# A decoder block on one core: the next group's front traced ahead of the recurrence's loop, adaLN's rows tied to chain operations with a third buffer, and loads respread

## The chip, the cores and the metric

The kernel runs on one core of a Trainium2 chip. The core's engines run side by side and meet only through semaphores: TensorE (PE in the profile, with its weight loads as PEld) multiplies matrices from SBUF into PSUM, VectorE (DVE) and ScalarE (ACT) do elementwise work, GpSimd (POOL) does some elementwise work off to the side, and SyncE (SP) issues every DMA of this kernel from one queue. The metric is the device time of one execution in microseconds. Before the change it is 2329.66 us, the median of three runs from 2323.95 to 2334.65.

## What is computed

One decoder block on x of 512 tokens by 2048 channels, all in float32. A normalised input, scaled and shifted by adaLN rows of a condition vector c, goes through one input projection into two mixers: an RWKV-7 recurrence over 16 heads of 64, and causal pooling with windows 2, 4, 8 and 16. Both outputs meet in one output projection. A gated MLP with a short convolution follows, and a last norm.

```python
mod = c_act @ w_ada[l] + b_ada[l]
sh1, sc1, gt1, sh2, sc2, gt2 = jnp.split(mod[:, None, :], N_MOD, axis=-1)
h = _rmsnorm(x, norm1_g[l]) * (1.0 + sc1) + sh1
p = h @ w_in[l]
y_rwkv = _rwkv7_mixer(p[..., :N_RWKV_COLS], ...)
y_pool = _pool_mixer(p[..., N_RWKV_COLS:], pool_w[l], pool_b[l], pool_scale[l])
mix = jnp.concatenate([y_rwkv, y_pool], axis=-1) @ w_out[l]
x = x + gt1 * mix
h = _rmsnorm(x, norm2_g[l]) * (1.0 + sc2) + sh2
x = x + gt2 * _conv_ffn(h, w_up[l], conv_w[l], conv_b[l], w_down[l])
```

## The kernel before

Activations lie transposed, 128 channels by 512 tokens to a tile. Weights and activations are split into a high part (`whi`, cast by ACT, line 122) and a remainder (`wlo`, subtracted by DVE, line 124), and a product is three matmuls (lines 128 to 130). Weights pass through four shared buffers `wraw`.

**The opening.** Sixteen steps over the channels project the pool inputs, sixteen more (`feed`, line 260) project eight tiles into the eight PSUM banks `pf`: one for the decay and rate inputs (`xwa`), two for the gate (`xg`), and five of the first r, k and v tiles. Lines 280 to 301 apply the token shift to each (`shift`: an ACT copy with a scale, then a DVE multiply and add) and take tanh and sigmoid of the first three. When the `pf` banks are free, their space becomes the banks of the recurrence: two single ones (`mm`), two double ones (`bt`) and a double one (`ch`).

**The recurrence.** The 16 heads go in four groups g of four heads. For each group:

- `front` (406): decay and rate from `xwa` (lines 420, 421), sigmoids, a scan, exponentials, and the norm of the keys.
- `rest` (462), a generator that stops at each `yield`. Its first part makes the operands `ar`, `bt`, the masked scores `sb` and `sk` (lines 485, 544), the token-major copies, and a small triangular solve on DVE (lines 556 to 566) whose result comes back through DRAM into `X`. The second part has two level steps (584 to 605: product, mask `pm`, add into `X`, add into `Y`), then the chain of eight dependent steps (620 to 649), then `y`. The third part, the tail, normalises `y`, applies the gate (lora weights `lg` and `gw`, 681 to 693) and stores two mix tiles.

While a group runs, PE fills its time with the input projection of the next group's six tiles (`win_some`, 703): r, k and v for two column tiles each. Each is shifted into a buffer `spill`, stored to DRAM, and reloaded by `load_cells` (716) when its place is free. Also in between are the pool groups (`pool`, 312), with weights `pw`, and 24 adaLN rows per group (`ada_rest`, 372): each is a 512 KB load into a tile `war` and one DVE product with a sum (line 381). Each of 48 rows is taken in two halves, which makes 96 products in all.

**Order.** Every instruction has a priority by its place in the source; `tc.high_priority` raises that of a block (the recurrence by 100000, pools and fronts by 50000). A scheduler lays out each engine's order before the kernel runs, taking at each time the ready instruction of highest priority. `in_step` (113) ties an adaLN row to an earlier instruction: it may not be placed ahead of it. Before, that is the last matmul of a projection block (`beats`), spread evenly over the group's blocks.

**After the recurrence.** The fourteen mix tiles that are ready are loaded and split (`load_mix`, 765) into the places of the normalised input H, the first ten output tiles are projected from them (772 to 782), and when the last group has its two mix tiles the rest follows with the residual (`x2` loads in 867 to 870, `residual` in 821).

## Time and profile before

| | |
|---|---|
| runs (three) | 2323.95, 2329.66, 2334.65 us |
| profiled execution | 2332.65 us, its span 2330.9 us |
| PE busy | 2202.7 us (95%) |
| PE weight loads | 1878.0 us (81%) |
| DVE busy | 1512.6 us (65%) |
| ACT busy | 925.9 us (40%) |
| POOL busy | 403.3 us (17%) |
| HBM read, written | 364.56 MB, 34.09 MB |

The span is the time from the first to the last instruction that the profile shows; the execution's own time is 1.75 us more. Opening, recurrence with output projection, and MLP follow one another: the four recurrence groups lie between about 215 and 730 us, the output projection's first stage goes to 795. A matmul's end is modelled, so busy shares of PE are an upper view, and its idle time is the surer reading.

### The profile page before, as it was taken

The numbers are of one execution on the slowest core, as the hardware profiler recorded it, in microseconds if no ns is written. First come the engines' busy times: TensorE is split into PE (matmuls) and PEld (weight loads), VectorE is DVE, ScalarE is ACT, GpSimd is POOL, SyncE is SP. The second block draws the span as 40 slices with busy tenths as digits, with TensorE's granted clock in tenths as the row PEclk, the third lists the DMA queues.
The fourth block names the chain that finished last, engine by engine and source line by source line (L and its number), as shares of the span: only waits on it lengthen the run. The fifth ranks groups of instructions, "written<-read, shape, count | busy, mean of one in ns | idle before, by whom it ended". The sixth has DMA issues, their size and how long they took to land.

```text
span 2330.9 us, 41813 instructions
## 1 busy us (share of the span) xinstructions
PE 2202.7 (95%) x16306; PEld 1878.0 (81%) x16306; DVE 1512.6 (65%) x2536; ACT 925.9 (40%) x1551; POOL 403.3 (17%) x390
## 2 busy tenths in 40 slices
PE   7999898888879898999999999999999999999997
PEld 5776666565657798899999999999999788888887
DVE  7896767685865669776656666656666444464457
ACT  4435242332523255544344434443444333343333
POOL 0000000000000005634434333344343000000000
PEclk9999999999989999999999999999999999999999
DMA  9884556566655775433333333333333766666555
GB/s 348 301 307 132 164 181 184 166 202 197 209 177 171 266 224 166 149 108 119 123 109 123 109 115 112 110 117 122 109 122 105 232 202 200 198 199 205 163 165 177
DMA packets 197465, 401.41 MB, mean 172 GB/s; under 512 B 37521, under 2 KB 49553, under 8 KB 193041
## 3 DMA queue, kind: packets, MB, share of 16 engines
q1 hardware_dynamic: 197266, 398.73, 54.0%
q8 instruction: 128, 2.10, 0.4%
q14 instruction: 71, 0.58, 0.1%
HBM read 364.56 MB, written 34.09 MB: 171 GB/s over the span
## 4 chain that ended last, share of the span: by engine, by line
PE 60%; DVE 2%; DMA 2%; ACT 0%; issue 0%; SPq 0%; DVEq 0%; ACTq 0%
PE b L130 20%; PE b L128 20%; PE b L129 20%; DVE wlo L124 1%; DMA wraw<-wdn 1%; DMA wraw<-wout 1%; DVE hl L159 0%; DVE x L1089 0%; ACT whi L122 0%; DVE acc L819 0%; DMA ald<-actd 0%; DVE h L157 0%; DMA x<-part 0%; DMA x<-x2d 0%; DVE x L823 0%
## 5 line engine op out<-in xcount | busy, mean ns | idle before, releaser
L122 ACT CAST whi<-wraw 128x512 fp32r<-128x512 f32 (+1 forms) x594 | 360.4, 609 | 820.8 <-DMA wraw<-wup 254.8
L124 DVE TENSOR_TENSOR wlo<-wraw,whi 128x512 fp32r<-128x512 f32 (+1 forms) x578 | 406.5, 705 | 270.9 <-ACT whi L122 263.1
L128 PE MATMUL b<-ah,whi 128*128 128x512 f32 (+1 forms) x980 | 350.0, 357 | 8.2 <-ACT whi L122 7.3
L130 PE MATMUL b<-ah,wlo 128*128 128x512 f32 (+1 forms) x980 | 349.5, 357 | 6.0 <-DVE wlo L124 5.8
L129 PE MATMUL b<-al,whi 128*128 128x512 f32 (+1 forms) x980 | 348.7, 356 | 0.0
L130 PE MATMUL b<-hh,wlo 128*128 128x512 f32 (+1 forms) x640 | 237.8, 372 | 6.0 <-DVE wlo L124 5.8
L128 PE MATMUL b<-hh,whi 128*128 128x512 f32 (+1 forms) x640 | 238.2, 372 | 0.0
L129 PE MATMUL b<-hl,whi 128*128 128x512 f32 (+1 forms) x640 | 237.8, 372 | 0.0
L128 PEld LDWEIGHTS b<-ah,whi 128*128 128x128 f32 x980 | 186.0, 190 | 36.6 <-ACT whi L122 10.8
L130 PEld LDWEIGHTS b<-ah,wlo 128*128 128x128 f32 x980 | 186.0, 190 | 34.4 <-DVE wlo L124 7.7
L129 PEld LDWEIGHTS b<-al,whi 128*128 128x128 f32 x980 | 186.1, 190 | 26.0
L984 DVE TENSOR_TENSOR pl<-raw,ph 128x768 fp32r<-128x768 f32 x104 | 105.4, 1014 | 153.0 <-ACT ph L983 153.0
L128 PE MATMUL mm<-ah,whi 128*128 128x512 f32 x444 | 183.3, 413 | 10.1 <-ACT whi L122 10.1
L130 PE MATMUL mm<-ah,wlo 128*128 128x512 f32 x444 | 183.8, 415 | 3.2 <-DVE wlo L124 3.2
L129 PE MATMUL mm<-al,whi 128*128 128x512 f32 x444 | 182.4, 411 | 0.0
L972 POOL TENSOR_TENSOR sums<-sums,raw 128x256 f32<-128x256 f32 x104 | 107.5, 1033 | 417.0 <-DVE sl L984 411.1
L130 PE MATMUL b<-tk,sl 128*128 128x256 f32 x624 | 176.7, 283 | 0.0
L129 PE MATMUL b<-tk,sh 128*128 128x256 f32 x624 | 176.5, 283 | 0.0
L128 PE MATMUL b<-tk,sh 128*128 128x256 f32 x624 | 176.0, 282 | 0.0
L983 ACT CAST ph<-raw 128x768 fp32r<-128x768 f32 x104 | 86.3, 830 | 165.9 <-PE b L129 159.5
L381 DVE SCALAR_TENSOR_TENSOR war<-war,cq 128x1024 f32<-128x1024 f32 x96 | 116.9, 1220 | 47.3 <-DMA war<-ada 47.2
L971 POOL TENSOR_TENSOR sums<-raw 128x512 f32<-128x512 f32 x104 | 135.8, 1305 | 66.9 <-DMA raw<-wups 33.1
(277 smaller groups left out, 4699.8 us busy)
## 6 DMA issues: line engine op xcount, KB each, us to landing
raw<-wups SPq DMA_DIRECT2D x104, 512.0 KB, 3.5
war<-ada SPq DMA_DIRECT2D x96, 512.0 KB, 4.4
wraw<-wdn SPq DMA_DIRECT2D x192, 256.0 KB, 3.2
wraw<-wup SPq DMA_DIRECT2D x160, 256.0 KB, 3.6
wa<-ada SPq DMA_DIRECT2D x32, 1024.0 KB, 7.5
wraw<-win SPq DMA_DIRECT2D x108, 256.0 KB, 4.1
ald<-actd SPq DMA_DIRECT2D x88, 256.0 KB, 2.7
wraw<-wout SPq DMA_DIRECT2D x78, 256.0 KB, 4.2
```

The lines of the kernel that those rows point to most:

```text
L122: mark[0] = S.copy(hi[:, 0:w], raw[:, 0:w]).ins
L124: mark[1] = eng.tensor_tensor(lo[:, 0:w], raw[:, 0:w], hi[:, 0:w].bitcast(F32), op=ALU.subtract).ins
L128: PE.matmul(ps, wh, xh, start=start, stop=False)
L129: PE.matmul(ps, wh, xl, start=False, stop=False)
L130: return PE.matmul(ps, wl, xh, start=False, stop=stop)
L381: op = V.scalar_tensor_tensor(wa, wa, 1.0, cq[0], op0=ALU.mult, op1=ALU.mult, accum_out=modq[:, kq, j : j + 1])
L971: G.tensor_tensor(sa, raw[:, 1:3, :], raw[:, 0:1, :].to_broadcast([P, 2, W2]), op=ALU.add)
L972: G.tensor_tensor(sb2[:, 0, :], sa[:, 0, :], raw[:, 2, :], op=ALU.add)
L983: act = S.copy(hi[:, sl, :], t)
L984: dve = V.tensor_tensor(lo[:, sl, :], t, hi[:, sl, :].bitcast(F32), op=ALU.subtract)
```

## The change

1. All eight shifts come first, tanh after the fourth; sigmoids and casts of the gate inputs follow when the banks are released.
2. `front` is cut in two, `front` and `key_norm`. A new `yield` in `rest` stands ahead of the chain's eight steps, and the next group's front is traced there. Of the next group's projections k comes first, then r, then the loads of both, and v is traced behind the chain.
3. In the last group that projects (g = 2), `win_two` projects both v tiles together, four channel tiles of the one and then of the other, and shifts them from PSUM straight into V. Twelve mix loads are traced right behind `win_two`, the last two behind the tail.
4. An adaLN row is tied to a DVE operation of its own group's recurrence instead of to a projection block: `spots` collects one to four places at each of the front's subtraction, the key norm, the masks, the triangular solve, the level masks, seven chain steps, and the tail. The `war` tiles have three buffers.
5. `spill`, `lg` and `rc` have one buffer where they had two; the pool weights lie in the places of `lg` and `gw` instead of in a `war` buffer.
6. Each residual tile `x2` is loaded behind the projection that needs it, instead of sixteen in a row ahead of the first.

```diff
+            for i in range(2):
+                shift(pf[1 + i], 25 + i, xg[:, i, :])
+            for i, (t, x, m) in enumerate(((0, 0, 0), (1, 0, 8), (2, 0, 16), (0, 1, 1), (1, 1, 9))):
+                shift(pf[3 + i], m, two(rkv0[t])[:, x, :])
+                if i == 0:
+                    S.activation(xwa[0:64, :], xwa[0:64, :], AF.Tanh)
+            ps0ctx.close()
...
+            def sigmoids():
+                for i in range(2):
+                    S.activation(xg[:, i, :], xg[:, i, :], AF.Sigmoid)
+                    S.copy(xgh[i], xg[:, i, :])
...
-        t = ra.tile([P, 2 * T], F32, tag="war", name="pw", bufs=2)
...
+        pw = [ra.tile([P, 2, P], F32, tag="lg", name="pw"), ra.tile([P, 3, P], F32, tag="gw", name="pw")[:, 0:2, :]]
+        for i in range(2):
+            nc.sync.dma_start(pw[i], a["poolw"][gi, :, i, :].rearrange("p (d w) -> p d w", d=2))
...
+    spots = [[] for _ in range(NQ)]
...
+        for n, spot in zip(range(n0, n1), spots[n0 // 24]):
...
-            wa = ra.tile([P, 2 * T], F32, tag="war", name="war", bufs=2)
+            wa = ra.tile([P, 2 * T], F32, tag="war", name="war", bufs=3)
...
-            i = at + (n - n0) * b // (n1 - n0)
-            if i < len(beats):
-                in_step(op, beats[i])
-        first_beat[0] = len(beats)
+            in_step(op, spot)
...
+        sb, dve = scores("b", bt)
+        spots[g] += [dve.ins] * 2
...
+        spots[g] += [dve.ins] * 2
         psb = batch()
...
+        dve = V.tensor_copy(xyl[:, 0, :, :], xyl[:, 1, :, :].rearrange("p i j -> p j i"))
+        spots[g] += [dve.ins] * 4
...
+            dve = V.tensor_tensor(rows(pm), wide(ps).rearrange("p (s t) -> p s t", t=C),
                             mlev[:, lev : lev + 1, :].to_broadcast([P, 2 * NK, C]), op=ALU.mult)
+            spots[g].append(dve.ins)
...
         S.copy(flat(xv), wide(ps))
+        yield
...
+                R = ra.tile([P, 2, C], F32, tag="rc", name="rc")
+                dve = V.tensor_add(R, pc[:, :, 0:C], xv[:, :, c, :])
+                spots[g].append(dve.ins)
...
+            lw = ra.tile([P, 2, P], F32, tag="lg", name="lg")
...
+    def win_two(pairs, i):
+        pss = [mmtile() for _ in pairs]
+        for k0 in range(0, KT, WC // P):
+            k1 = k0 + WC // P
+            for p, ps in zip(pairs, pss):
+                project(ps, a["win1"][3 + 3 * p + i - 8, :, k0 * P : k1 * P], H[k0:k1], start=k0 == 0, stop=k1 == KT)
+        return pss
...
+        if more:
+            win_some(pairs, (0,))
+            with lower():
                 r, k = load_cells(g + 1, (0, 1))
         with hp():
             next(quad)
+        if more:
+            with lower():
+                fr = key_norm(g + 1, k, front(g + 1))
+        with hp():
+            next(quad)
+        if g < NQ - 2:
+            win_some(pairs, (2,))
+        elif more:
+            pss = win_two(pairs, 2)
+            with lower():
+                for i in range(NM - 2):
+                    load_mix(i)
         with hp():
             next(quad, None)
+            if more:
+                if g < NQ - 2:
+                    rkv = [r, k] + load_cells(g + 1, (2,))
+                else:
+                    v = cell("V", "v")
+                    for x in range(2):
+                        shift(pss[x], 16 + pairs[x], two(v)[:, x, :])
+                    rkv = [r, k, v]
+        if g == NQ - 2:
+            with lower():
+                for i in range(NM - 2, NM):
+                    load_mix(i)
...
-    for i in range(NM):
-        load_mix(i)
...
+    def load_x2(f):
         t = rx.tile([P, T], F32, tag=f"x2_{f}", name=f"x2_{f}")
         nc.sync.dma_start(t, part[f] if f < NW else a["xT"][:, f, :])
         x2.append(t)
+
     for f in range(NW):
         ps = bank()
         project(ps, a["wout"][f, :, NM * P :], M[NM:])
+        load_x2(f)
         residual(f, ps, mod[:, 32 + f : 33 + f], acc, 0, T, f == 0)
```

## The prediction

> **What bounds the kernel now.** I began with the page (PE busy for 95% of the span), then cut the span into stages with the view of windows, to see where TensorE (PE) is not busy. The columns are the stretch, its length, then busy time and instructions of PE, its weight loads, DVE, ACT and POOL, the granted clock, the DMA share and GB/s.

> ```profile
> 205.00:215.00 10.00, 5.38 (x20) 1.45 (x19) 5.95 (x9) 8.67 (x15) 0.95 (x1) 0.83 0.06 16
> 215.00:730.00 515.00, 447.39 (x5974) 322.04 (x5974) 354.52 (x649) 184.13 (x310) 2.86 (x3) 0.95 0.59 179
> 730.00:795.00 65.00, 65.00 (x286) 53.23 (x284) 43.33 (x73) 18.82 (x34) 0.00 (x0) 1.00 0.73 235
> 795.00:820.00 25.00, 17.64 (x71) 13.69 (x71) 17.20 (x31) 10.46 (x21) 0.00 (x0) 0.86 0.80 274
> ```

> The change touches only what lies between 205 and 820. There PE idles 4.62 us at the switch from the input projections to the recurrence, 515.00 - 447.39 = 67.61 us in the four recurrence groups, nothing from 730 to 795, and 7.36 us where the residual tiles are loaded: 79.6 us. Outside those holes PE works, so the change can only gain what it takes out of these 79.6 us. The view of waits for PE between 205 and 820 says who ended the holes (total, times, longest):

> ```profile
> PE mm L128 <- ACT whi L122: 10.1, 2, 9.8
> PE bt L588 <- DVE X L599: 8.7, 3, 3.7
> PE bt L656 <- DVE Y L605: 7.1, 4, 2.7
> PE bt L483 <- DVE ar L475: 6.2, 3, 3.4
> PE b L130 <- DVE wlo L124: 4.5, 1, 4.5
> PE bt L420 <- DVE r L269: 4.5, 1, 4.5
> PE bt L495 <- DVE sb L485: 4.5, 3, 1.5
> PE bt L531 <- DVE sb L485: 4.0, 4, 1.1
> PE bt L495 <- DMA v<-sp: 2.8, 2, 2.0
> ```

> Most of it is DVE: a matrix product stands at the head of PE's queue, its operand comes late from DVE, and the projection work behind it can't pass. Each term below is one of these rows.

> **Part 1, adaLN's rows (three buffers, tied to chain operations).** This row of the page is the load of a row's product on DVE:

> ```profile
> L381 DVE SCALAR_TENSOR_TENSOR war<-war,cq 128x1024 f32<-128x1024 f32 x96 | 116.9, 1220 | 47.3 <-DMA war<-ada 47.2
> ```

> 96 rows of 1.22 us, and 47.2 us in which DVE stands still at a row whose 512 KB have not landed. What that does is seen in the level step of the first group (timeline: start, length, instruction, and in brackets the idle time before it and what ended it):

> ```profile
> 283.38 0.28 PE L597 MATMUL bt<-pm,Y 64*64 64x64 f32 x2
> 283.45 2.08 PE L603 MATMUL bt<-Y,pm 64*64 64x64 f32 x63
> 284.21 1.23 DVE L381 SCALAR_TENSOR_TENSOR war<-war,cq 128x1024 f32<-128x1024 f32 x1 [4.99 <-DMA war<-ada]
> 285.53 1.23 DVE L381 SCALAR_TENSOR_TENSOR war<-war,cq 128x1024 f32<-128x1024 f32 x1
> 286.68 1.22 DVE L599 TENSOR_TENSOR X<-X,bt 128x1024 f32<-128x1024 f32 x1
> 287.95 0.29 PE L588 MATMUL bt<-X,sb 64*64 64x64 f32 x4 [2.43 <-DVE X L599]
> ```

> The add into X needs only the L597 products, which end at 283.66, so it could run from about 283.9 to 285.1, under the L603 products that last to 285.53. Two rows stand ahead of it and PE loses 2.43 us. The change allows one row behind each mask operation pm, where DVE's next step waits for PE anyway, and a third buffer lets its load be asked for earlier. The L588 and L656 rows hold 8.7 + 7.1 = 15.8 us. All of it can't go, because the last add into Y (1.22 us) must precede L656 in any order, so I take three quarters: **-12**, with ends 0 (the rows clump elsewhere as they do now) and -15.8.

> The same spots add work where DVE is short. Two rows follow the last mask of sb and two that of sk, four times: 16 rows of 1.3 us (1.22 and the 0.08 of reading the sum) or 20.8 us at worst. The rows for L495 and L531 (8.5 us) show that PE already waits there for DVE. Since the rows are of lowest priority and DVE's order is laid out in advance around them, I take **+3**; ends 0 and +20.8. Queued behind such a row are the next masks and the splits wlo, and PE waits for both.

> The 96 loads stay at 512 KB each on SP's single queue, so its bytes don't change. A third buffer lets an issue wait less often for a product; I count nothing for it beyond the -12. If it fails, that -12 goes too.

> **Part 2, eight shifts first.** Today tanh, two sigmoids, two casts and two table loads stand on ACT between the third and fourth shift:

> ```profile
> 202.72 1.28 ACT L282 ACT_TABLE_LOAD   x1
> 204.01 0.63 ACT L282 ACTIVATE xwa<-xwa 64x512 f32<-64x512 f32 x1
> 208.04 0.68 ACT L268 ACTIVATE r<-pf,drv 128x512 f32<-128x512 f32 x1
> 209.88 1.21 PE L420 MATMUL bt<-xwa,lw 64*64 64x512 f32 x2 [4.51 <-DVE r L269]
> 210.41 0.74 DVE L269 SCALAR_TENSOR_TENSOR v<-pf,vec,v 128x511 f32<-128x511 f32 x1
> ```

> L420 waits for the bank that r's shift frees, L421, issued between the L420 products, for that of v's shift, which ends at 211.15. With r fourth, then tanh (1.28 + 0.63), then k and v at 0.68 each, v's DVE half ends near 207.3. Front's sixteen products end 3.9 us sooner: **-4**, ends -2 and -4.6. The sigmoids and casts go behind the shifts, beside front's own sigmoids, and cost nothing there: xg is first read in the first group's tail, after the chain of 300 to 325.

> **Part 3, front ahead of the loop, and r and k earlier.** Front of group g+1 is now traced after the chain of group g; the change traces it before the chain's eight steps, at lower priority. Its first instance shows its length as a serial chain, 226.30 - 214.60 = 11.7 us, and two windows show the chain of group 0 and the front behind it:

> ```profile
> 214.60 1.27 ACT L424 ACTIVATE sg<-bt,vec 128x512 f32<-128x512 f32 x2 [1.32 <-PE bt L421]
> 224.88 1.42 DVE L458 SCALAR_TENSOR_TENSOR inv<-k,vec,inv 128x512 f32<-128x512 f32 x2 [0.27 <-ACT inv L456]
> 300.00:325.00 25.00, 24.18 (x374) 14.97 (x374) 15.13 (x38) 9.25 (x26) 0.00 (x0) 1.00 0.58 184
> 325.00:345.00 20.00, 20.00 (x164) 13.40 (x156) 14.35 (x20) 16.17 (x22) 0.95 (x1) 1.00 0.40 128
> ```

> Behind the chain PE is busy for all of 20.00 us, so projections already cover front. Moving it saves no hole by itself; what it shortens is the recurrence's path. Under the chain DVE is busy for 15.13 of 25 us and ACT for 9.25, so there is room, but a chain copy or add of 0.3 us can find a long scan or exponential ahead of it in its queue. I take 2 us for each of three groups, **+6**, with ends 0 (projections fill PE) and 3 x 11.7 = +35.

> With r's and k's projections ahead of the chain, their loads from DRAM land sooner. The DVE view beside the PE rows gives the load of r:

> ```profile
> DVE ar L475 <- DMA r<-sp: 4.4, 2, 3.3
> ```

> Those two are the 3.4 and one of the others in the L483 row: **-4.5**, ends 0 and -6.2.

> **Part 4, last v tiles in place, and the mix loads under them.** Today all fourteen mix tiles come after the last projection, and the new projection's weights come after them in the shared wraw buffers:

> ```profile
> 609.03 1.22 DVE L693 TENSOR_TENSOR rs<-rs,bt 128x1024 f32<-128x1024 f32 x1
> 656.63 0.62 ACT L151 CAST ah<-mxl 128x512 fp32r<-128x512 f32 x1 [0.73 <-DMA mxl<-mixd]
> 658.51 0.62 ACT L122 CAST whi<-wraw 128x512 fp32r<-128x512 f32 x1 [1.27 <-DMA wraw<-wout]
> 659.18 0.79 PE L128 MATMUL mm<-ah,whi 128*128 128x512 f32 x1 [9.77 <-ACT whi L122]
> 660.00:665.00 5.00, 5.00 (x13) 3.96 (x13) 3.28 (x13) 1.64 (x3) 0.00 (x0) 0.53 0.71 204
> 665.00:670.00 5.00, 5.00 (x23) 4.13 (x22) 3.70 (x7) 0.62 (x1) 0.00 (x0) 1.00 0.84 258
> ```

> Two tiles projected chunk by chunk release H's slots over two tiles' time instead of one, so twelve mixes can be split before the projections run out. Two mixes still come from the tail of group 2. Of 9.77 us I take **-7**, ends 0 and -9.8. At a granted clock of 0.53 the window after the hole passes 13 products against 23, 10 x 0.22 = 2.2 us: **-1.5** of it goes with the hole. [...]

> The last v needs no store and reload: **-2** of the 2.8 us that L495 waits for v, ends 0 and -2.8. The two mm banks stay taken until group 2's tail has released V. No projection can use them then; if the tail were late, PE would idle. The tail's last product stands at 609.03 and the mixes follow the projections with casts to 656.63, so V is free in time, and I cost that at nothing.

> **Part 5, residual loads spread.** Sixteen loads of x stand in SP's queue before the next weights, the last six for 4.75 us:

> ```profile
> 803.48 4.75 SPq L869 DMA_DIRECT2D x<-xT  x6
> 810.74 0.50 PE L130 MATMUL b<-ah,wlo 128*128 128x512 f32 x1 [4.54 <-DVE wlo L124]
> ```

> The wlo that ends the 4.54 us hole sat behind residual adds on DVE that had waited for x. Spread, the weights go ahead; but ten residual pairs of about 1.3 us still meet PE steps of 1.4 us. **-3.5**, ends 0 and -6.5 (with the 1.9 us hole behind it).

> **Part 6, single buffers.** The spill, the lora tile lg and rc lose their second buffer, pool weights move to lg and gw.

> ```profile
> sp<-spill SPq DMA_DIRECT2D x18, 256.0 KB, 3.0
> lg<-lora SPq DMA_DIRECT2D x5, 128.0 KB, 2.6
> ```

> A spill's store of 3.0 us lies inside the next tile's 48 products (48 x 0.22 = 10.6 us): nothing. Of a pair of lora loads the second now waits for the first's readers, 2.6 us in the tail under projections: **+1** over four groups, ends 0 and 4 x 2.6 = +10.4. Cover gone, it is the whole 10.4. The pool products' own wait for a mm bank is left as it is: 0.

> **The sum.** -12 - 4 - 4.5 - 7 - 1.5 - 2 - 3.5 = -34.5, and +3 + 6 + 1 = +10: -24.5 against the profiled execution's own 2332.65, so 2308.2. That execution lay 3.0 above the median of the runs, 2329.66, so against the runs I say **2305**.

> **The rivals.** *The holes stay, with other names* (18%). The orders of DVE and PE are set in advance, and a late row still holds up what stands behind it; rows pile up at sb and sk as they do now at X, and only Parts 2, 4 and 5 pay: -4 - 7 - 1.5 - 2 - 3.5 + 3 = -15, or 2315; with half of Part 4 lost, 2320. For it: L495 and L531 already wait for DVE. Against it: the biggest single waits are row waits that a third buffer shortens. This is also the case in which the edits don't do what they say.

> *The single buffers show* (6%). If PE has nothing else ready when lg's second load or a spill's store is out, 10.4 us and 16 spills of perhaps 0.5 us are lost: 2305 + 18 = 2323. The windows speak against it, PE being full behind the chain. [...]

> *DVE becomes the bound of the recurrence* (8%). Front's 35 us and the 20.8 us of rows at sb and sk would all push the chain while PE stands behind it: 56 us, of which the sum holds 9, so 2305 + 47 = 2352 at the full price. It is slower than before once more than 34 of the 56 us show as PE idle. For it: chain steps of 0.3 us queue behind 2 us scans. Against it: 24.18 of 25 us busy in the chain, with DVE free 40% of the time.

> *Nearly every hole closes* (8%): parts at their far ends, about -45, or 2285.

> **Chances.** The forecast, 2295 to 2316, has 60%. About 0.5% is what a measurement of this kernel can tell from no change, so faster means below 2318 and slower above 2341. Faster: 60 + 8 + some of the first rival = 76%; same 16%, slower 8%. The range, 2283 to 2326, takes in the far ends and the first two rivals.

> **What would show it.** Right: L588 and L656 waits under 6 us together, DVE's wait for adaLN loads under 20 us, L420 issuing before 206, the mm hole near 650 under 4 us, scan and exponentials between chain steps, the chain still about 25 us long. Wrong: the chain longer by over 5 us a group, L495 or L531 waits doubled, a hole at the first out-projection, or weight loads waiting at SP behind adaLN rows.

## The result, and the profile after

The changed kernel takes 2316.18 us, the median of six runs from 2312.78 to 2320.96, against 2329.94 us, the median of six runs of the kernel before, taken beside them. The ratio is 0.9944 with a 95% interval of 0.9925 to 0.9963: faster by 0.6%, or 13.8 us, where the prediction had said 24.5. The profiled execution has a span of 2311.4 us, 19.5 below that of before.

The view of windows of the changed kernel, cut at the stages that the prediction used (columns as there):

```profile
203.80:215.00 11.20, 6.74 (x25) 2.71 (x26) 8.07 (x10) 11.15 (x18) 0.95 (x1) 0.92 0.11 28
215.00:716.00 501.00, 446.24 (x5973) 321.36 (x5972) 363.84 (x675) 180.90 (x306) 2.86 (x3) 0.96 0.62 193
716.00:780.00 64.00, 64.00 (x278) 51.88 (x279) 30.01 (x50) 19.75 (x33) 0.00 (x0) 1.00 0.45 136
780.00:806.00 26.00, 21.49 (x107) 16.81 (x106) 18.48 (x33) 12.36 (x23) 0.00 (x0) 1.00 0.77 256
```

The holes of PE are now 4.46 + 54.76 + 0 + 4.51 = 63.7 us, against 79.6 before. These windows do not hold quite the same work (the last has 107 PE products, that of before 71). Whole sections compare best from the last product into `pf` to the first product of the output projection's second stage; each of these two lines is one kernel's, before and after:

```profile
205.40:796.00 590.60, 517.47 (x6277) 376.77 (x6277) 404.71 (x734) 211.48 (x357) 3.81 (x4) 0.96 0.59 182
```

```profile
203.80:781.70 577.90, 517.76 (x6276) 376.28 (x6277) 402.89 (x736) 212.20 (x357) 3.81 (x4) 0.96 0.59 183
```

The section is 12.7 us shorter, all of it idle PE (73.1 to 60.1 us). Of the rest of the 19.5 us, 1.6 lie ahead of the section, 0.9 in the residual stage behind it and 4.2 in the MLP. In the first and the last of these nothing was changed, so they are taken as the scatter of one execution.

The waits of PE in the section (total, times, longest) say that the holes were traded more than closed. Lines have moved: 588 is now 598, 656 is 669, 483 is 490, 495 is 502, 531 is 539, 420 is 418, 599 is 610.

```profile
PE bt L598 <- DVE X L610: 13.4, 4, 3.8
PE bt L502 <- DMA v<-sp: 6.6, 4, 2.3
PE bt L688 <- ACT rs L685: 4.7, 3, 1.9
PE bt L490 <- DVE ar L482: 4.4, 2, 2.7
PE bt L502 <- DVE sb L492: 4.0, 4, 1.6
PE bt L457 <- ACT sg L422: 3.6, 1, 3.6
PE bt L457 <- ACT inv L456: 3.0, 2, 2.3
PE bt L502 <- DVE v L269: 2.1, 2, 1.6
PE bt L539 <- DVE sb L492: 1.8, 3, 0.6
...
PE bt L418 <- DVE Y L616: 1.4, 3, 0.6
...
PE mm L128 <- ACT whi L122: 1.0, 1, 1.0
...
PE bt L669 <- DVE Y L616: 0.7, 1, 0.7
...
PE bt L418 <- DVE r L269: 0.7, 1, 0.7
```

The hole ahead of the output projection is gone (10.1 to 1.0 us), and the wait behind the last add into Y fell from 7.1 us to 2.1: 0.7 at the old place (L669), and 1.4 at L418, the next group's front, which now stands there in three groups. The wait behind the add into X, the largest target of Part 1, grew from 8.7 to 13.4. DVE's wait for the adaLN loads was halved (47.2 before, 22.0 now, in the view of groups):

```profile
L383 DVE SCALAR_TENSOR_TENSOR war<-war,cq 128x1024 f32<-128x1024 f32 x96 | 116.1, 1218 | 24.0 <-DMA war<-ada 22.0 <-DMA cq<-cact 1.9
```

But what is left of it stands in the worst place. The timeline of the first group's level step:

```profile
282.80 1.85 PE L614 MATMUL bt<-Y,pm 64*64 64x64 f32 x56
285.57 1.23 DVE L383 SCALAR_TENSOR_TENSOR war<-war,cq 128x1024 f32<-128x1024 f32 x1 [4.93 <-DMA war<-ada]
...
286.72 1.22 DVE L610 TENSOR_TENSOR X<-X,bt 128x1024 f32<-128x1024 f32 x1
...
287.99 1.84 PE L598 MATMUL bt<-X,sb 64*64 64x64 f32 x64 [3.33 <-DVE X L610]
```

The row behind the mask `pm` would fit in the time in which DVE waits for PE, if its 512 KB were there. They are not: DVE stands for 4.93 us at that row, the add into X behind it starts late, and PE loses 3.33 us. It is so in all four groups (the row 4, 3.8 the longest). A little earlier four rows are tied to the end of the triangular solve and use up the loaded tiles, and SP's queue is then taken by the eight small loads of X and, up to 279.58, by a store and by loads of weights and of k, ahead of the next row's:

```profile
266.74 0.42 SPq L382 DMA_DIRECT2D war<-ada  x1
267.44 5.37 SPq L582 DMA_DIRECT2D X<-dxy  x8
```

### The profile page after: what moved, and what is told of

It is laid out like the page before. It is cut to its first block, busy times and chain, and to the rows that moved or that the text cites. A ratio compares the mean times of both kernels' runs of the same rounds, so it can differ in the third digit from the quotient of the medians.

```text
span 2311.4 us, 41801 instructions
## 1 busy us (share of the span) xinstructions
PE 2200.9 (95%) x16306; PEld 1874.1 (81%) x16306; DVE 1508.7 (65%) x2536; ACT 925.2 (40%) x1551; POOL 408.5 (18%) x390
## 4 chain that ended last, share of the span: by engine, by line
PE 54%; DMA 1%; DVE 1%; ACT 0%; issue 0%; SPq 0%; DVEq 0%; ACTq 0%
PE b L128 18%; PE b L130 18%; PE b L129 18%; DMA wraw<-wdn 1%; DMA ald<-actd 0%; DVE x L1139 0%; DMA x<-x2d 0%; DVE wlo L124 0%; SPq L1119 0%; DVE al L152 0%; ACT whi L122 0%; ACT ah L151 0%; PE b L178 0%; DVE sl L1034 0%; DVE x L868 0%
## 5 line engine op out<-in xcount | busy, mean ns | idle before, releaser
L122 ACT CAST whi<-wraw 128x512 fp32r<-128x512 f32 (+1 forms) x594 | 360.8, 609 | 849.3 <-DMA wraw<-wup 253.2
L124 DVE TENSOR_TENSOR wlo<-wraw,whi 128x512 fp32r<-128x512 f32 (+1 forms) x578 | 406.1, 705 | 292.2 <-ACT whi L122 286.4
L128 PE MATMUL b<-ah,whi 128*128 128x512 f32 (+1 forms) x980 | 348.9, 356 | 8.1 <-ACT whi L122 7.2
L130 PE MATMUL b<-ah,wlo 128*128 128x512 f32 (+1 forms) x980 | 348.7, 356 | 3.9 <-DVE wlo L124 3.3
L130 PE MATMUL b<-hh,wlo 128*128 128x512 f32 (+1 forms) x640 | 236.6, 370 | 5.4 <-DVE wlo L124 5.4
L128 PE MATMUL b<-hh,whi 128*128 128x512 f32 (+1 forms) x640 | 237.2, 371 | 0.1
L128 PEld LDWEIGHTS b<-ah,whi 128*128 128x128 f32 x980 | 185.2, 189 | 36.8 <-ACT whi L122 11.4
L130 PEld LDWEIGHTS b<-ah,wlo 128*128 128x128 f32 x980 | 185.1, 189 | 33.4 <-DVE wlo L124 7.0
L129 PEld LDWEIGHTS b<-al,whi 128*128 128x128 f32 x980 | 185.2, 189 | 25.6
L128 PE MATMUL mm<-ah,whi 128*128 128x512 f32 x444 | 183.1, 412 | 1.4 <-ACT whi L122 1.0
L130 PE MATMUL mm<-ah,wlo 128*128 128x512 f32 x444 | 181.1, 408 | 1.1 <-DVE wlo L124 1.1
L130 PE MATMUL b<-tk,sl 128*128 128x256 f32 x624 | 176.7, 283 | 0.5 <-DVE sl L1034 0.5
L128 PE MATMUL b<-tk,sh 128*128 128x256 f32 x624 | 176.0, 282 | 0.0
L130 PEld LDWEIGHTS b<-hh,wlo 128*128 128x128 f32 x640 | 120.6, 188 | 28.9 <-DVE wlo L124 7.9
## 6 DMA issues: line engine op xcount, KB each, us to landing
wraw<-wdn SPq DMA_DIRECT2D x192, 256.0 KB, 3.3
wraw<-wup SPq DMA_DIRECT2D x160, 256.0 KB, 3.6
wraw<-win SPq DMA_DIRECT2D x108, 256.0 KB, 4.2
ald<-actd SPq DMA_DIRECT2D x88, 256.0 KB, 2.7
wraw<-wout SPq DMA_DIRECT2D x78, 256.0 KB, 3.9
```

Of the source, the lines that this page charges most:

```text
L122: mark[0] = S.copy(hi[:, 0:w], raw[:, 0:w]).ins
L124: mark[1] = eng.tensor_tensor(lo[:, 0:w], raw[:, 0:w], hi[:, 0:w].bitcast(F32), op=ALU.subtract).ins
L128: PE.matmul(ps, wh, xh, start=start, stop=False)
L129: PE.matmul(ps, wh, xl, start=False, stop=False)
L130: return PE.matmul(ps, wl, xh, start=False, stop=stop)
```

## The experiments

Each is the changed kernel with one edit, or with several of these edits together; e9 and e15 leave work out and do not compute the block. The table gives the medians, the ratio to the kernel before measured beside it, and the difference from the changed kernel by the two ratios, times 2330 us. Half-widths of 0.0019 and 0.0017 combine to 0.0025, so a difference carries about 6 us either way. Every edit also lays out the orders of all engines anew: the medians of the ten runs that compute the block lie between 2306.69 and 2320.75 us, so a difference between two of them is the price of an edit in that order, not of a mechanism by itself.

| run | median us | ratio, 95% interval | to the changed kernel, us |
|---|---|---|---|
| changed kernel | 2316.18 | 0.9944 (0.9925 to 0.9963) | |
| e1 no row at the first mask | 2313.24 | 0.9936 (0.9919 to 0.9953) | -1.9 |
| e2 gate sigmoids behind the front | 2318.23 | 0.9953 (0.9936 to 0.9970) | +2.1 |
| e3 both of these | 2319.41 | 0.9964 (0.9949 to 0.9978) | +4.7 |
| e4 rows on projection blocks | 2307.69 | 0.9912 (0.9893 to 0.9930) | -7.5 |
| e5 front behind the chain | 2306.69 | 0.9913 (0.9896 to 0.9930) | -7.2 |
| e6 v behind r | 2309.79 | 0.9919 (0.9901 to 0.9937) | -5.8 |
| e7 residual loads in one burst | 2320.75 | 0.9963 (0.9949 to 0.9977) | +4.4 |
| e8 as e4, two buffers | 2315.69 | 0.9949 (0.9931 to 0.9967) | +1.2 |
| e11 as e4 and e5 | 2318.29 | 0.9959 (0.9945 to 0.9974) | +3.5 |
| e13 as e4, e5 and e6 | 2316.60 | 0.9951 (0.9933 to 0.9968) | +1.6 |
| e9 no adaLN rows | 2279.86 | 0.9787 (0.9767 to 0.9808) | -36.6 |
| e15 their products without their loads | 2276.94 | 0.9784 (0.9767 to 0.9802) | -37.3 |

**One row away from the level step (e1).** If the row behind `pm` is what holds the add into X, no row may stand there.

```diff
-            spots[g].append(dve.ins)
+            if lev:
+                spots[g].append(dve.ins)
```

> The changed kernel, but with no adaLN row tied to the first level mask of a group (the group's last free place behind the tail takes a row instead). Theory: in all four groups this row stands in DVE's order right ahead of the add into X, its load is late because the four rows behind the solve have used all three buffers, and PE waits 13.4 us in total for that add. Then the wait of the level products for X falls from 13.4 us to under 3 us, DVE's wait for adaLN loads from 22 to under 8 us, and the time falls by 8 to 11 us against the changed kernel (to about 2306). Rival (PE's holes only move, since the recurrence as a whole sets the pace): the wait for X falls as said but another wait rises by as much and the time stays within 3 us of the changed kernel.

The waits of PE, with the add into X now at line 611:

```profile
PE bt L598 <- issue: 6.0, 2, 3.2
PE bt L598 <- DVE X L611: 3.6, 1, 3.6
PE bt L615 <- issue: 3.5, 2, 3.1
```

The wait for the add fell as wanted, from 13.4 to 3.6 us, and the time did not follow. In the same places, in the middle of the 64-wide products of the level step, PE now waits for nothing that the profile shows ("issue"). The time came out as the rival said: with the first cause of the hole gone, another stands there. What that is comes in the last section.

**The opening (e2, e3).** In the opening the front's first products now start early, but the row sg L422, 3.6 us, is new. The timeline of the changed kernel shows why: table load, gate sigmoids and casts have moved behind the shifts, and so ahead of the front's own sigmoid.

```profile
206.53 1.28 ACT L298 ACT_TABLE_LOAD   x1
207.82 1.15 ACT L298 ACTIVATE xg<-xg 128x512 f32<-128x512 f32 x2
...
209.49 1.12 ACT L299 CAST xgh<-xg 128x512 fp32r<-128x512 f32 x2
...
211.56 1.25 ACT L422 ACTIVATE sg<-bt,vec 128x512 f32<-128x512 f32 x2
...
212.86 1.86 PE L457 MATMUL bt<-inv,cmat 128*128 128x512 f32 x2 [3.57 <-ACT sg L422]
```

e2 puts the gate's sigmoids behind the front's last exponential, e3 does this and e1's edit together.

```diff
-            sigmoids()
...
+    with tc.issue_after(last_exp[0]):
+        sigmoids()
```

> The changed kernel, but with the gate's two sigmoids and two casts behind the first front's last exponential on ACT. Theory: at the opening of the recurrence they stand ahead of front's own sigmoids, so that the eight shifts gain nothing; PE's wait of 3.6 us for the first front's sigmoid falls under 1 us and the key norm product starts about 3 us sooner; the time falls by 2 to 4 us, which is at the edge of what is measured. Rival: the key norm product then waits as long for the square or for the shift of k, and the time does not change.

> The edits of the two runs before together. Theory: the holes add up, so the time is 10 to 14 us below the changed kernel (about 2303 to 2306) and PE's idle time between 205 us and the first product of the output projection's second stage falls from 58 to about 46 us. Rival: both gains are given back in other holes and the time is within 4 us of the changed kernel.

The wait for sg fell to 1.5 us, and in the profiled execution the level step's waits grew to 14.1 us for X and 3.6 of issue. Neither run is faster than the changed kernel, and e3 has none of the 10 to 14 us that its theory wanted. The 2 us that the wait for sg lost can't be seen in a difference that carries 6 us, so whether that hole reaches the end is not shown.

**Rows on projection blocks (e4), and with two buffers (e8).** e4 undoes the tie to chain operations and keeps the third buffer; e8 undoes both.

```diff
-        for n, spot in zip(range(n0, n1), spots[n0 // 24]):
+        b, at = len(beats) - first_beat[0], first_beat[0]
+        for n in range(n0, n1):
...
-            in_step(op, spot)
+            i = at + (n - n0) * b // (n1 - n0)
+            if i < len(beats):
+                in_step(op, beats[i])
+        first_beat[0] = len(beats)
```

> The changed kernel, but with the adaLN rows tied to projection blocks as before the change, with the third buffer kept. Theory: what the third buffer and the chain spots do for the adds into Y and for the first masks is worth little net (the rows' waits fell by 25 us on DVE, but PE's waits for X and Y only from 15.8 to 14.1): slower than the changed kernel by 2 to 7 us. Rival: the row places are where most of the 14 us came from, and without them the time is within 4 us of the kernel before (10 us or more above the changed one).

> adaLN's rows behind projection blocks, as in the kernel before, and two buffers for them instead of three; against the run with projection blocks and three buffers (2307.69 us). Theory (DVE runs ahead of the loads with either count, and its 18.8 us of waits for them stand in stretches that PE does not wait for): within 2 us, 2306 to 2310 us. Rival (the third buffer is what makes the rows cheap): DVE's wait for the loads goes from 18.8 to 40 us or more, the level steps and the scores wait as before the change, and the time is 2312 to 2318 us.

e4 is faster than the changed kernel, against both expectations: the tie to chain operations loses some 7 us against the old pacing here. The waits of PE behind the add into X are 5.4 us there. e8 gives these 8 us back. In the view of groups DVE's waits for the adaLN loads are 34.6 us in e8 and 18.8 in e4. So with rows on projection blocks the third buffer gains about 8 us, and the chain spots then lose about as much. e8 is the changed kernel without Part 1, and only 1.2 us slower: that is what Part 1 as a whole is worth, within 6 us.

**The front behind the chain (e5).**

```diff
         with hp():
             next(quad)
+            next(quad)
         if more:
             with lower():
                 fr = key_norm(g + 1, k, front(g + 1))
-        with hp():
-            next(quad)
```

> The next group's front is traced behind the chain's last step again; all else is as changed. Theory (the forecast's Part 3, the front's 64 PE instructions and its DVE and ACT rows fill holes of the chain): the chains of the first three groups come back from 29.6, 32.2 and 31.2 us to about 26, the front stands alone behind them, and the time rises by 4 to 6 us, to 2320 to 2322 us. Rival (the front only takes the chain's place, what it gains behind the chain it costs in the chain): within 2 us of the changed kernel, 2314 to 2318 us.

Both missed: the time fell, by 7.2 us. The windows of the first three chains, from the first copy of `ua` to the last, in the changed kernel and then in e5:

```profile
297.90:327.50 29.60, 28.97 (x417) 17.40 (x421) 21.95 (x46) 17.96 (x36) 0.00 (x0) 1.00 0.48 150
416.60:448.80 32.20, 30.78 (x420) 18.86 (x422) 23.01 (x48) 19.94 (x39) 0.00 (x0) 1.00 0.53 156
549.80:581.00 31.20, 28.36 (x388) 16.87 (x392) 21.43 (x47) 18.10 (x36) 0.00 (x0) 1.00 0.50 153
```

```profile
296.30:319.90 23.60, 23.25 (x395) 14.43 (x399) 15.94 (x39) 9.03 (x25) 0.00 (x0) 1.00 0.55 177
414.90:439.30 24.40, 24.09 (x385) 14.92 (x389) 16.30 (x40) 9.07 (x25) 0.00 (x0) 1.00 0.60 183
543.80:568.10 24.30, 23.95 (x402) 14.99 (x405) 16.44 (x41) 8.94 (x26) 0.00 (x0) 1.00 0.52 163
```

Under the chain the front adds some 6 us of DVE and 9 us of ACT work, and each chain is 6 to 8 us longer. There was next to nothing to fill: without the front PE is idle for 0.35 us of the 23.60. Behind the chain the front's work lies beside the tail's, and the waits for rs (4.7 us) and inv (3.0 us), which the changed kernel has, do not appear among the waits of e5.

**v behind r (e6), residual loads in one burst (e7).**

```diff
-            win_some(pairs, (0,))
+            win_some(pairs, (0, 2) if g < NQ - 2 else (0,))
...
-        if g < NQ - 2:
-            win_some(pairs, (2,))
-        elif more:
+        if g == NQ - 2:
```

> For the second and third group v's column tile is projected right behind r's, as in the kernel before; the fourth group's v in place stays. Theory (v's projection now ends last, and its way over a spill and a load is on the path): the wait of PE at L502 for the load of v, 6.6 us, falls under 2 us, and the time falls by about 5 us, to 2311 us. Rival (v's products are the filler of a hole behind the chain, which then shows under another name, at the output's rows or in the front): within 2 us, 2314 to 2318 us.

```diff
+    for f in range(KT):
+        load_x2(f)
     for f in range(NW):
...
-        load_x2(f)
```

> The sixteen residual loads are issued in one burst ahead of the output projection's second stage again. Theory (the forecast's Part 5, where the profiles show 7.36 against 4.51 us of idle PE in that stage): about 3 us more, 2319 us, with PE waits of the residual stage near 7 us. Rival (the loads were hidden, and the difference is of one execution): 2314 to 2317 us.

e6 has the expected gain, 5.8 us, but it is no larger than its uncertainty, and not by the expected way: the wait for v's load is 5.6 us, hardly below the 6.6. That the time came out as forecast is luck. e7 is 4.4 us slower, also within the uncertainty. Of its waits in the residual stage this one is the largest:

```profile
PE b L130 <- DVE wlo L124: 4.3, 1, 4.3
```

It is the wait behind one wlo that the kernel before had with 4.5 us. In the changed kernel the same row has 1.6 us in four waits, 0.9 the longest. From the first product of the second stage to the first product into `acc` the stage is 64.2 us long before, 63.3 in the changed kernel and 64.5 in e7, so only 1.2 us of e7's difference lies where the edit is.

**What the rows cost in all (e9, e15).** e9 leaves out the loop's 96 adaLN loads and products, e15 the loads alone.

```diff
-        for n, spot in zip(range(n0, n1), spots[n0 // 24]):
+        for n, spot in ():
```

```diff
-            nc.sync.dma_start(wa, a["ada2"][kq, j, :, :])
-            op = V.scalar_tensor_tensor(wa, wa, 1.0, cq[0], op0=ALU.mult, op1=ALU.mult,
+            op = V.scalar_tensor_tensor(wa, wone, 1.0, cq[0], op0=ALU.mult, op1=ALU.mult,
```

> The changed kernel with all 96 adaLN rows of the loop left out, their loads of 512 KB and their DVE products, and with zeros in their place in the sums; so the scale, shift and gate of adaLN are not computed in full, and the time is one without that work. It gives the price of rows and loads together, and tells whether they or the front make the chain long. Theory (the front under the chain is what lengthens it, and the rows cost only at the level step and in the queue of loads): the chains of the first three groups stay within 1.5 us of 29.6, 32.2 and 31.2, the 13.4 us of PE waits for the level step's add (L610) go under 3 us, and the time is 2302 to 2308 us. Rival (the rows among the chain's adds lengthen it, and their loads crowd the queue): the chains fall under 27.5 us, and the time under 2300 us.

> The changed kernel with the 96 loads of adaLN's rows left out and their 96 DVE products kept, at the same places, on a tile of ones; so adaLN's sums are not those of its weights. It splits the 36 us between the changed kernel (2316.18 us) and the run with neither loads nor products (2279.86 us). Theory (the loads are dear: DVE's row waits for them ahead of the level step's add, and 48 MB in the queues delay the loads of X and v and PE's own instruction blocks): 2280 to 2292 us, the PE waits for the level step's add (L610, 13.4 us) under 6 us, the waits put down to issue under 3 us. Rival (the products are dear: 96 times 1.2 us of DVE ahead of adds and copies that PE needs): 2304 to 2316 us, with 10 us or more of PE waits for that add.

This settles most of it. Without loads and products the time is 2279.86 us; with the products back, at the same spots, 2276.94. Without the loads, the 96 products, 116 us of DVE, cost nothing that can be measured. The 96 loads cost 37 us. Both times are under the ranges of the theories (2302 and 2280 us): e9's rival was right about the time, and e15's theory about which of the two is dear. e15's section, in the view of windows:

```profile
204.90:748.40 543.50, 503.82 (x6277) 368.15 (x6277) 402.81 (x736) 212.36 (x357) 3.82 (x4) 0.99 0.35 105
```

DVE does the same 403 us of work as in the changed kernel. What differs is the DMA share, 0.35 against 0.59, and with it idle PE (39.7 against 60.1) and the granted clock (0.99 against 0.96). The waits of PE for the add into X are gone from the view; what stays at the level step is mostly the unnamed kind, 5.0 us in all, where the theory wanted under 3:

```profile
PE bt L599 <- issue: 4.0, 3, 1.8
```

Most other transfers land sooner too; v's loads (2.8 to 3.6 us) and the lora loads (lg 2.4 to 2.5, lw 1.9 to 2.3) are the exceptions. Three rows of the DMA view (KB each, median us to landing), of the changed kernel and then of e15:

```profile
k<-sp SPq DMA_DIRECT2D x6, 256.0 KB, 4.7
mixd<-rs SPq DMA_DIRECT2D x6, 256.0 KB, 4.0
...
X<-dxy SPq DMA_DIRECT2D x32, 16.0 KB, 2.4
```

```profile
k<-sp SPq DMA_DIRECT2D x6, 256.0 KB, 3.1
mixd<-rs SPq DMA_DIRECT2D x6, 256.0 KB, 2.0
...
X<-dxy SPq DMA_DIRECT2D x32, 16.0 KB, 2.0
```

The runs show two ways in which the loads can cost: a row's product stands on DVE until its load lands and holds what is behind it (22.0 us of DVE's waits in the changed kernel), and other transfers land later (k's loads in 4.7 us with them, 3.1 without). No run kept the loads and left out the products, so how the 37 us divide between these is open.

e9 also answers its own question: its chains are 28.3, 25.6 and 27.6 us long, where the theory wanted them within 1.5 us of 29.6, 32.2 and 31.2; in e15, with products and without loads, they are 30.2, 31.1 and 27.8. So the products lengthen some chains, and even so cost the end nothing.

**Gains that don't add (e11, e13).**

> Both edits that were faster than the changed kernel: adaLN's rows behind projection blocks (alone 8.5 us less) and the front behind the chain (alone 9.5 us less). Theory (two separate prices, one at the chain, one at the level steps and in the loads): they add, 2296 to 2300 us. Rival (one price, DVE crowded by front and rows together under the chain, which either edit removes): 2304 to 2308 us, as with one of them.

> As the run with both edits, and v's column tile projected right behind r's (alone 6.4 us less than the changed kernel). Theory (the wait for v's load, 6 to 7 us in each run so far, is on the path whatever stands beside it): 4 to 6 us under the run with both edits. Rival (with the front behind the chain, the products of v are wanted there as cover): within 2 us of it, or above.

e4 and e5 are each some 7 us faster than the changed kernel; both edits together are not (+3.5), and 10.7 us slower than e5 alone, which is beyond the uncertainty. Neither theory nor rival of e11 had that. e13 is 1.9 us under e11, as its rival said; the wait for the load of v, on which its theory rested, does not appear in e11 at all and is 3.4 us in e13. e11's waits of PE begin with a row that has 1.1 us in the changed kernel and 5.3 in e5:

```profile
PE mm L130 <- DVE wlo L124: 9.3, 6, 3.0
PE bt L602 <- DVE X L614: 6.5, 3, 4.0
PE bt L506 <- DVE sb L496: 5.9, 4, 1.5
PE bt L554 <- DVE sk L556: 4.7, 2, 4.3
```

PE now waits for DVE's part of the split of a projection's weights. The table divides the section into idle PE, the clock lost (for each stretch of 10 us its length times one minus the granted clock), and a rest of 491 to 497 us, whose scatter of 6 us none of this explains.

| kernel | section | idle PE | clock lost | rest |
|---|---|---|---|---|
| before | 590.6 | 73.1 | 25.5 | 492.0 |
| changed | 577.9 | 60.1 | 22.1 | 495.7 |
| e4 | 569.3 | 54.0 | 20.6 | 494.7 |
| e5 | 567.4 | 51.5 | 22.1 | 493.8 |
| e11 | 579.3 | 55.6 | 27.3 | 496.4 |
| e9 | 544.1 | 39.4 | 13.6 | 491.1 |
| e15 | 543.5 | 39.7 | 6.8 | 497.0 |

Against e5, e11 has 4.1 us more idle PE, 5.2 more of lost clock and 2.6 more of rest. Why its order of DVE work falls out so was not tried; it stays open. The fastest versions that compute the whole block are e5 and e4, at 0.9913 and 0.9912 of the time before.

## Why the prediction was right and wrong

The direction was right, and for the named reason: PE's holes between 205 and 820 were the only thing to gain, and what was gained is idle PE. The size was about half, and the terms missed in both directions, and some of the misses cancelled.

- **Part 1, adaLN's rows: -12 forecast, -0.3 seen in the waits named, -1.2 in time by e8.** The waits for X and Y went from 15.8 to 13.4 + 0.7 + 1.4 = 15.5 us. What did fall at the level step is something else: the unnamed waits (5.0 us) and those for `pm` (3.1) of the kernel before come to 0.2 us in the changed one. This is the step that failed. The prediction took the rows' place in DVE's queue for the cause and gave the third buffer no worth of its own. e4 and e8 say the reverse: the buffer gains about 8 us and the new places give about as much back. This holds with the front under the chain; with the front behind it (e5 and e11) the new places are the better ones, by 10.7 us. e9 and e15 say what is dear: 1.2 us of DVE at a spot is free once its load is not awaited, and the loads are not. The prediction noted that the bytes in SP's queue don't change, and counted nothing for that. It was the line with the 37 us in it, and both kernels pay them.
- **Rows at sb and sk: +3 forecast.** The two rows named for it went from 8.5 to 4.0 + 1.8 = 5.8 us; the waits for sk went from 2.2 to 3.0. No cost.
- **Part 2, eight shifts first: -4 forecast, -0.2 seen.** L418 went from 4.5 to 0.7 us, and the products issued at 204.45, as said. The working then put the sigmoids and casts "beside front's own sigmoids" at nothing, and they stand ahead of them on ACT: 3.6 us at L457. e2 removed most of that, and a gain of its size is too small to see in the time.
- **Part 3, front under the chain: +6 forecast.** By e5 it costs 7 us, with an uncertainty of 6; with the rows on projection blocks (e4 and e11) it gains 11 instead. The mechanism was as described, scans and exponentials among chain steps. The sign of being wrong, "the chain longer by over 5 us", came true in one of the three groups against the kernel before (26.2, 25.1 and 28.0 us there, so 3.4, 7.1 and 3.2 longer), and in all three against e5. **r and k earlier: -4.5 forecast**; the row for ar went from 6.2 to 4.4, so -1.8. DVE's wait for the load of r, which was to go, stayed: 4.4 us before, 4.2 now.
- **Part 4, the output projection's first hole: -7 forecast, -9.1 seen.** This is the clearest gain of the change, read from the waits; no run took it back alone. **v in place: -2 forecast, +5.9 seen**: the waits for v went from 2.8 to 6.6 + 2.1 us. The prediction saw the fourth group's v, which is no longer stored, and passed over the second and third, whose v is now projected last and needed soon after. **Clock: -1.5 forecast**, lost clock 25.5 to 22.1.
- **Part 5, residual loads: -3.5 forecast, -0.9 seen** in the length of the whole stage (64.2 to 63.3 us), with 1.5 us less idle PE in it. The 7.36 and 4.51 us of idle PE in the windows of 25 and 26 us do not compare, as they hold 71 and 107 products. e7 has the sign, +4.4 us, not resolved from none.
- **Part 6, single buffers: +1 forecast.** PE's waits under the name of spill fell from 4.2 us to 1.1, those under rc stayed at 0.7, and lg has none. The tail's waits for rs (4.7 us) are new, and with the front moved (e5) they go. At these three tiles the loss of the second buffer made no longer wait of PE; the adaLN stream gains 8 us by one buffer more, between e8 and e4.

The rival nearest to the outcome was "the holes stay, with other names", at 2315 to 2320: the median of 2316.18 lies in it, and it is just outside the forecast's own 2295 to 2316. Its mechanism, rows piling up at sb and sk, is not what happened; the rows piled up at the triangular solve and the level step. The new waits that no term had are those for sg, inv and rs (3.6 + 3.0 + 4.7 us) and v's 5.9 us more.

## What to carry to other kernels

When an engine waits for a streamed operand, price the stream by two runs, one without the transfers and one without transfers and arithmetic, before arranging where the arithmetic goes: here the arithmetic without the transfers was free, and the transfers cost 37 us. A third run, with transfers and no arithmetic, would have told how they cost it. A slot in which an instruction fits is worth something only if its data has landed by then (here DVE stood for 4.93 us at a row of 1.23 us), so pace consumers with the loads' landing times, and don't spend several loaded buffers just ahead of the tight place (no run here tried such a pacing). Where every engine's order is laid out in advance, gains of single edits don't add: each is to be measured together with the others, as e11 showed against e4 and e5.

## What the runs showed of the hardware

**What a hole costs in clock goes by windows of 3.41 us.** The stretch that holds the first level step's hole, 3.33 us in the changed kernel and 1.80 us in e15, has its granted clock in the third column from the end:

```profile
285.00:295.00 10.00, 7.01 (x187) 6.10 (x191) 7.66 (x10) 1.21 (x2) 0.00 (x0) 0.83 0.46 161
```

```profile
285.00:295.00 10.00, 8.23 (x178) 5.71 (x177) 4.06 (x6) 1.39 (x3) 0.00 (x0) 1.00 0.01 3
```

The stretch with the hole of 3.33 us has 0.83, that with the hole of 1.80 us has 1.00. But the length of a single hole does not decide it. In e15 the clock stands at 0.50 from 359.58 to 363.00, behind a hole of 2.06 us, and from 615.58 to 618.99, behind two holes of 1.44 and 0.50 us; in the 3.41 us ahead of each, PE is busy for 1.35 and 1.47 us:

```profile
356.17:359.58 3.41, 1.35 (x36) 0.95 (x34) 1.91 (x9) 0.00 (x0) 0.00 (x0) 1.00 0.65 204
359.58:363.00 3.42, 3.42 (x16) 2.16 (x8) 3.12 (x11) 0.59 (x2) 0.00 (x0) 0.50 0.28 77
...
612.16:615.57 3.41, 1.47 (x28) 0.79 (x26) 3.39 (x9) 2.44 (x4) 0.00 (x0) 1.00 0.66 208
615.58:618.99 3.41, 3.41 (x73) 2.89 (x74) 2.55 (x8) 0.97 (x2) 0.00 (x0) 0.50 0.60 190
```

PE's busy time does not follow the lost clock alone. The changed kernel and e15 pass the same products in the section, 6276 and 6277, in 517.76 and 503.82 us, and their lost clock differs by 15.3 us; but e9 needs 504.69 us with twice e15's lost clock, and the kernel before 517.47 with 3.4 us more than the changed one.

**An instruction queue moves by DMA in step with PE, and PE's unnamed waits end behind its packets.** The profile's page of the changed kernel has this queue,

```profile
q8 instruction: 128, 2.10, 0.4%
```

which makes 16 KB a packet. The profile names no engine for it, but the packets keep step with PE's work: the page counts 16306 products and as many weight loads of PE, 255 for each of the 128 packets, and in the trace PE begins 252 of them between the starts of two packets in the median (195 to 303 in the middle 80% of the gaps; DVE begins 19, and 5 to 32). The trace has 48 of these packets between 205 and 745 us in the changed kernel, 1.1 us each. In e1 the level step's hole of 3.18 us began at 283.2, the packet started at 283.94 and landed at 284.87, and PE went on at 286.37. In e15 the hole of 1.80 us began at 284.23, with the packet started at 283.65 and landed at 284.60, and PE went on at 286.03. So PE resumed 1.50 and 1.43 us behind the landing.

It is so wherever PE waits like this: between 200 and 800 us the fourteen traces have 31 waits of PE of 1 us or more that the view puts down to "issue", 3.6 us the longest, and each of them ends 1.2 to 1.6 us behind the landing of such a packet, although the packets come only every 11 us. So the author takes these unnamed holes for waits for instructions; the traces show the order of the two events, not the cause. Most packets end no such hole, as there are at most five in a kernel and some 50 packets. That the adaLN loads make packets late is a guess of the author's: in e9 and e15 the packet had started before each of their three holes began, in the other kernels in 15 of 28. These are few, and no run changed the instruction stream alone, so that part is not shown.
